# Seven products for all of the output projection: operand sums on GpSimd, weight sums by adding DMAs

## The chip, the cores and the metric

The kernel runs on one core of a Trainium2 chip. The metric is the device time of one execution in microseconds (us), as the median of several runs. The core has five engines that run their own instruction streams and meet at semaphores: TensorE (PE in the profile; its weight loads are listed apart as PEld) multiplies matrices into PSUM, VectorE (DVE) and ScalarE (ACT) work on tiles in SBUF and PSUM, GpSimd (POOL) does elementwise work and issues DMAs, and SyncE (SP) issues DMAs only. A DMA moves data between device memory (DRAM) and SBUF, or from DRAM to DRAM; an accumulating DMA adds what it reads to what stands at its destination.

## The reference

One layer of a decoder on 512 tokens with 2048 channels, all in fp32. Two mixers work on the normalised input, A (sparse attention) and B (a gated MLP over chunks). The change lies behind them:

```python
merged = g_a * (o_a @ w_up_a[l]) + g_b * (o_b @ w_up_b[l])
x = x + merged @ w_out[l]                                            # the output projection
x = x + jax.nn.sigmoid(x @ w_ple_gate[l]) * (p[l] @ w_ple[l])
return rms_norm(x, final_g)
```

`merged` is 512 x 2048 and `w_out` 2048 x 2048.

## The kernel before, in words

**Precision.** Each fp32 operand is held as two parts, a rounded one ("high", made by ACT at L147) and the rest ("low", the subtraction on VectorE at L153). A product of two operands is three matmuls: high by high, high by low, low by high.

**Jobs.** All large matrix products are jobs of one list, and the generator `gemm()` works through them in the order of the list, one matmul group at a time. `fill(n)` lets it do n groups, `finish(name)` lets it run until that job is done; between such calls the program text issues other work (loads, transposes, stores). There are plain jobs (kinds "T" and "N") and jobs of kind "S", which compute a product of 2 x 2 blocks in seven block products instead of eight (Strassen's scheme). In an "S" job of the projection's size the blocks are: two halves of the tokens, two halves of the 2048 inputs (16 k-tiles of 128, so 8 per half), and two column blocks of 512 that start at `c0` and `c2`. The products are named "1" to "7". Each needs a sum or difference of blocks of the activations (by `sum_part` for products 5, 6, 3, and with a third sum for product 7; the text calls them first, second, third and fourth sums) and of the weights (for products 5, 7, 6 and 4). Their results are added in PSUM banks where they can be, and on VectorE where not.

I call a *piece* the 12 matmuls of one product and one pair of k-tiles: two k-tiles, two token tiles of 128, three matmuls each. A product of the projection has four pieces, an "S" job 28. The inner matmuls of an "S" job are L377 to L379, those of an "N" job L415 to L417.

**Order ahead of a piece.** Before each piece (or each pair of k-tiles of a plain job) `gemm()` calls `flush()`, which issues the work put off in `deferred`; then `split_to()`, which issues ACT's high and VectorE's low of the weights up to two pieces ahead (`state["ahead"]`, into rings of three tiles, `hs` and `ls`); then `pop()`, which takes steps from two queues: `background` (small pieces of vector work, at a rate of `state["pops"]` per piece) and `slow` (DMAs that sum weights in DRAM, at a rate of 0.6 per piece). Every engine executes its instructions in the order in which this program issues them; no scheduler reorders them.

**DMA queues.** SP's queue carries the weights alone, 512 KB each, into rings of 3, 4 and 4 buffers (`rings`: raw, b11, b12). All other transfers are issued on GpSimd's queue, between GpSimd's own work.

**The jobs in time.** The mixers' projections come first, with the attention (its scores from 220 to 474 us) in the same TensorE stream. Four jobs m0 to m3 (721 to 1038 us) make the merge gates from `w_in`, ua0/ua1 and ub0/ub1 (to about 1195 us) the two up-projections. ub0 and ub1 read weight sums from DRAM (`up_sums`), which 32 DMAs on GpSimd's queue have made early (`up_sum`, L1141 to L1157: a copy of one block, then an accumulating DMA of the other; from the `slow` queue). At the end of ub0 and ub1, `final_up` (L816 on VectorE, L817 on GpSimd) forms the merged rows.

**Around the change.** `turn_merged(i, banks, n)` (L1713, transposes at L1724) turns the merged rows of half i into the layout that the projection needs, in four steps of eight transposes; each step takes two PSUM banks by letter, gives their highs to ACT and their lows to VectorE (L155), and then lets `gemm()` do n groups. wo0 and wo1 are the "N" jobs of the projection's first 1024 columns, 512 each; their results are added to the residual x by `add_x` (L833). wo2 is an "S" job of the other 1024 columns; the differences of its weights are formed by VectorE (L271). The sums of its activations are made by `sum_chunk` (L1480) on VectorE, as background steps during wo0 and wo1; the third sums go to DRAM (`s3_dram`) and are read back by `load_s3`. As each 512 columns of the new x are done, `store_x2` writes them to DRAM and `turn_x2` transposes them for the next product with `w_ple_gate` (jobs pg0 to pg3). Two parts of the order, in the main sequence:

```python
    finish("ub1")
    fill(4)
    turn_merged(1, "gs", 4)
    ...
    finish("wo0")
    store_x2(0)
    fill(6)
    turn_x2(0, "to", stage, 8, third_sum(quad_places))
    load_x(1, new_x())
    finish("wo1")
```

## Time and profile before

| what | value |
|---|---|
| median of three runs | 1543.36 us (1542.88 to 1543.55) |
| the profiled execution | 1543.99 us, its span 1541.9 us |
| granted TensorE clock, mean | 0.998 |
| busy: PE / PEld / DVE / ACT / POOL | 1527.2 / 1278.5 / 1225.7 / 807.8 / 312.5 us |
| DMA | 298.61 MB, mean 194 GB/s |
| wo0 and wo1, 1194.9 to 1287.0 us: PE / DVE / ACT / POOL | 92.10 / 71.75 / 38.02 / 19.86 us of 92.10 |
| wo2, 1287.0 to 1366.9 us: PE / DVE / ACT / POOL | 79.83 / 64.03 / 37.76 / 11.98 us of 79.90 |

How to read it: the span runs from the first to the last instruction of one profiled execution; the execution's own time is 2.1 us longer. A busy time counts how long an engine executed instructions; matmuls overlap in TensorE's pipeline, so the duration of one (0.39 us) is longer than the distance to the next. Lines name an engine, a line of the kernel (often that of a helper such as `low`), the operation, and the tiles written and read. An arrow names what ended a wait.

### The profile page before, as it was taken

What the parts mean: (1) busy time and instruction counts of PE and PEld (TensorE: products, weight loads), DVE (VectorE), ACT (ScalarE), POOL (GpSimd) and SP (SyncE); (2) the same over time, 40 slices, a digit from 0 to 9 for tenths busy, and PEclk for the clock granted to TensorE, in tenths of its full rate; (3) what the DMA queues carried; (4) which work ended last, traced back from release to release, by engine and by line L of the source; (5) the groups of instructions that cost most, each with busy time, mean ns of one, the idle gap of its engine ahead of it and who ended that gap; (6) DMA issues with size and microseconds to landing.
All of it is one profiled execution on the core that took longest, in us unless ns stands there. A gap on an engine that the chain in (4) does not pass through costs nothing.

```text
span 1541.9 us, 20629 instructions
## 1 busy us (share of the span) xinstructions
PE 1527.2 (99%) x7390; PEld 1278.5 (83%) x7390; DVE 1225.7 (79%) x1901; ACT 807.8 (52%) x1369; POOL 312.5 (20%) x494
## 2 busy tenths in 40 slices
PE   9999999999999999999999999999999999999997
PEld 7889988888888888888888888888888888888886
DVE  6548758888887888978988787787888786978877
ACT  6534446666665555545545445455545343444556
POOL 1201121212223233301122132230123221100000
PEclk9999999999999999999999999999999999999999
DMA  8426754356548884917474646686875487454555
GB/s 311 143 82 189 232 132 112 103 106 171 118 138 225 285 283 133 287 55 245 150 276 132 237 137 231 223 275 237 296 291 177 137 264 228 157 198 167 188 205 191
DMA packets 175846, 298.61 MB, mean 194 GB/s; under 512 B 11240, under 2 KB 88704, under 8 KB 172544
## 3 DMA queue, kind: packets, MB, share of 16 engines
q1 hardware_dynamic: 117456, 157.96, 31.4%
q0 software_dynamic: 58144, 139.07, 29.7%
q8 instruction: 58, 0.95, 0.2%
q14 instruction: 44, 0.36, 0.1%
q10 hardware_dynamic: 144, 0.26, 0.0%
HBM read 235.91 MB, written 78.12 MB: 204 GB/s over the span
## 4 chain that ended last, share of the span: by engine, by line
PE 92%; DVE 4%; ACT 1%; issue 1%; DMA 1%; SPq 0%; POOL 0%; DVEq 0%; ACTq 0%; POOLq 0%
PE ps_m L378 6%; PE ps_m L379 6%; PE ps_m L377 6%; PE ps_za L403 2%; PE ps_t L1240 2%; PE ps_za L404 2%; PE ps_za L405 2%; PE ps_wo L417 2%; PE ps_wo L415 2%; PE ps_wo L416 2%; PE ps_pg L378 2%; PE ps_wo L378 2%; PE ps_pg L377 2%; PE ps_pg L379 2%; PE ps_ua L378 2%; PE ps_zb L379 2%
## 5 line engine op out<-in xcount | busy, mean ns | idle before, releaser
L153 DVE TENSOR_TENSOR ls<-b,hs 128x1024 fp32r<-128x1024 f32 x210 | 262.0, 1248 | 106.5 <-ACT hs L147 104.7
L147 ACT CAST hs<-b 128x1024 fp32r<-128x1024 f32 x210 | 220.7, 1053 | 239.3 <-PE ps_m L379 65.5
L153 DVE TENSOR_TENSOR lo<-raw,hi 128x512 fp32r<-128x512 f32 (+1 forms) x184 | 125.7, 689 | 55.2 <-issue 18.6
L147 ACT CAST hi<-raw 128x512 fp32r<-128x512 f32 (+1 forms) x184 | 109.1, 603 | 87.9 <-PE ps_wo L417 19.4
L147 ACT CAST hs<-raw 128x1024 fp32r<-128x1024 f32 x94 | 99.0, 1054 | 104.2 <-PE ps_m L379 28.6
L153 DVE TENSOR_TENSOR ls<-raw,hs 128x1024 fp32r<-128x1024 f32 x94 | 116.9, 1244 | 24.3 <-ACT hs L147 24.3
L377 PE MATMUL ps_m<-hs,act_h 128*128 128x512 f32 x256 | 100.5, 393 | 0.0
L378 PE MATMUL ps_m<-ls,act_h 128*128 128x512 f32 x256 | 99.9, 390 | 0.2 <-DVE ls L153 0.2
L379 PE MATMUL ps_m<-hs,act_l 128*128 128x512 f32 x256 | 99.7, 389 | 0.0
L271 DVE TENSOR_TENSOR b<-raw,b 128x1024 f32<-128x1024 f32 x80 | 97.4, 1218 | 2.1 <-DMA raw<-in_w_in_dram 1.5
L271 DVE TENSOR_TENSOR b<-b,b 128x1024 f32<-128x1024 f32 x80 | 97.4, 1218 | 0.0
L147 ACT CAST pth<-ps_t 128x512 fp32r<-128x512 f32 (+1 forms) x88 | 48.0, 545 | 65.7 <-PE ps_t L1240 65.4
L1201 ACT ACTIVATE prob<-prob,st 128x512 f32<-128x512 f32 (+3 forms) x128 | 70.7, 556 | 4.0 <-DVE st L1192 3.8
L153 DVE TENSOR_TENSOR ptl<-ps_t,pth 128x512 fp32r<-128x512 f32 (+1 forms) x88 | 56.1, 638 | 20.8 <-ACT pth L147 20.0
L1192 DVE CUSTOM_DVE_ANT_0 prob<-ps_s,b 128x512 f32<-128x512 f32 (+3 forms) x128 | 56.3, 486 | 9.9 <-PE ps_s L1189 9.7
L378 PEld LDWEIGHTS ps_m<-ls,act_h 128*128 128x128 f32 x256 | 48.1, 188 | 10.7 <-DVE ls L153 1.0
L379 PEld LDWEIGHTS ps_m<-hs,act_l 128*128 128x128 f32 x256 | 48.1, 188 | 10.0
L377 PEld LDWEIGHTS ps_m<-hs,act_h 128*128 128x128 f32 x256 | 48.1, 188 | 9.8
L403 PE MATMUL ps_za<-act_h,hi 128*128 128x512 f32 x128 | 55.8, 436 | 0.0
L403 PE MATMUL ps_q<-act_h,hi 128*128 128x512 f32 x128 | 53.6, 419 | 0.0
L1240 PEld LDWEIGHTS ps_t<-ident,prob 128*128 128x128 f32 x320 | 39.7, 140 | 13.9 <-DVE ptl L153 3.0
L1240 PE MATMUL ps_t<-ident,prob 128*128 128x128 f32 x320 | 49.4, 273 | 1.4 <-DVE ptl L153 1.3
(686 smaller groups left out, 4463.8 us busy)
## 6 DMA issues: line engine op xcount, KB each, us to landing
raw<-in_w_in_dram SPq DMA_DIRECT2D x112, 512.0 KB, 4.3
b<-in_w_in_dram SPq DMA_DIRECT2D x56, 512.0 KB, 5.5
t<-in_w_up_b_dram POOLq DMA_DIRECT2D x24, 512.0 KB, 7.3
raw<-in_w_out_dram SPq DMA_DIRECT2D x24, 512.0 KB, 3.8
raw<-in_w_ple_gate_dram SPq DMA_DIRECT2D x24, 512.0 KB, 3.8
act_l<-gate POOLq DMA_DIRECT2D x8, 1024.0 KB, 10.5
hsum<-h_stage POOLq DMA_DIRECT2D x12, 512.0 KB, 4.3
gate<-keep POOLq DMA_DIRECT2D x24, 256.0 KB, 3.7
```

Of the source, the lines that this page charges most:

```text
L147: nc.scalar.copy(hi, src)
L153: nc.vector.tensor_tensor(out=lo, in0=src, in1=hi.bitcast(F32), op=ALU.subtract)
L271: nc.vector.tensor_tensor(out=b[o], in0=b[x], in1=b[y], op=ALU.subtract)
L377: nc.tensor.matmul(o, ah, wh, start=st, stop=False, skip_group_check=go)
L378: nc.tensor.matmul(o, ah, wl, start=False, stop=False, skip_group_check=go)
L379: nc.tensor.matmul(o, al, wh, start=False, stop=sp, skip_group_check=go)
L403: nc.tensor.matmul(ps, hi[:, j], ah, start=st, stop=False)
L404: nc.tensor.matmul(ps, hi[:, j], al, start=False, stop=False)
L405: nc.tensor.matmul(ps, lo[:, j], ah, start=False, stop=sp)
L1192: nc.vector.tensor_tensor_reduce(out=pt[:, j * n:j * n + n], in0=o[:, j], in1=b0[:, 512 - n:], scale=-SLOPE[h], scalar=3.0e38, op0=ALU.add ...
L1201: nc.scalar.activation(sl, sl, AF.Exp, bias=st[:, 0, j, hh:hh + 1], scale=-1.0, accum_out=st[:, 1, j, hh:hh + 1])
L1240: nc.tensor.transpose(b[:, (2 * e + hh) * P:(2 * e + hh + 1) * P], pts[hh][:, c:c + P], ident)
```

## The change

The first 1024 columns of the projection are computed by seven products too. The jobs wo0 and wo1 become one "S" job wo0 with column blocks at 0 and 512, in an order of its own (`LATE`) and with four pairs of PSUM banks instead of three (`LATE_BANK`); since a bank may now be opened by any product, `gemm()` works out for each bank which product begins it. Products 1 and 2 come first, product 3 last.

Both projection jobs get `sums`: the weight sums are read from DRAM (`out_sums`). `weight_sum` replaces `up_sum` and makes them for ub0, ub1, wo0 and wo2, as 96 DMAs on GpSimd's queue instead of 32. They stand in the `slow` queue from earlier on, and are taken from it at a rate of 0.8 per piece early, none while the sums of h are made, 0.85 in the attention, then none again, and 0.34 in m0 to m3. VectorE's weight differences in wo2 (L271 of the kernel before) go.

The sums of the activations are made by `merged_sums` in place of `sum_chunk`. 28 operations of 128x512 run on GpSimd (`gp`): 8 for the whole rows (two of the four `whole` steps while ub1 ends, two in wo0), 4 third sums, 8 first and 8 fourth; VectorE keeps the four second sums and the lows of all the results. They are spread over wo0 by a table of its 28 pieces (`plan`). The store of the third sums and `load_s3` go.

The order of the program changes around it. `turn_merged(1)` stands after `fill(2)` and uses the two banks "o" in all four steps, where it used "g" and "s". `turn_x2(0)` moves from wo1 into wo2. The second quarter of x is held as four tiles, stored block by block at wo0's end, and read back from `x2_dram` for `turn_x2(1)`.

```diff
+        self.bank_of = bank_of or BANK_OF
+        self.begins = {b: next(p for p, _ in products(self) if self.bank_of[p] == b) for b in set(self.bank_of.values())
+                       } if kind == "S" else None
...
+LATE = [(p, j) for p, js in (("1", "0123"), ("2", "2301"), ("4", "012"), ("7", "012"), ("6", "0123"), ("7", "3"),
+                             ("5", "0123"), ("4", "3"), ("3", "0123")) for j in map(int, js)]
+LATE_BANK = {"1": 0, "7": 0, "6": 1, "5": 1, "3": 1, "2": 2, "4": 3}
...
     def pop():
-        state["late"] += 0.6
+        state["late"] += state["rate"]
...
-                    b = BANK_OF[p]
+                    b = job.bank_of[p]
+                    begins = job.begins[b] == p
+                    pieces = [i for q, i in products(job) if q == p]
+                    opens, closes = j == pieces[0], j == pieces[-1]
...
-    s3_dram = dram.tile([P, 2, 8, 256], F32R, name="s3_d")
+    out_sums = [{p: dram.tile([P, 8, 512], F32, name=f"o{p}{i}") for p in "5674"} for i in range(2)]
...
-    for cg in range(2):
-        add_job(Job(f"wo{cg}", "N", w_out, 512 * cg, 512, KT, h_act, evac_out(cg), (ys, xs)[cg]))
+    def evac_out(p, ps):
+
+        for cg, row in {"1": ((0, 0), (1, 0)), "2": ((0, 0),), "7": ((0, 2), (1, 2)), "4": ((0, 2),),
+                        "6": ((0, 2),), "5": ((1, 2),), "3": ((1, 0),)}[p]:
+            for t in range(2):
+                add_x(cg, row + t, ps[t])
+        if p == "4":
+            later(lambda: store_x2(0))
+        elif p in "53":
+            for t in range(2):
+                later(lambda t=2 * (p == "5") + t: nc.gpsimd.dma_start(x2_dram[block(t, 512)], x_tiles[1][t]))
+
+    add_job(Job("wo0", "S", w_out, 0, 512, KT, part_act, evac_out, ("t", "g", "s", "o"), order=LATE, bank_of=LATE_BANK,
+                sums=out_sums[0]))
     add_job(Job("wo2", "S", w_out, 1536, 512, KT, part_act,
-                evac_quad(lambda t, c, o, src: add_x(2 if c else 3, t, src), tiles=False), ("o", "t", "s"), c2=1024))
+                evac_quad(lambda t, c, o, src: add_x(2 if c else 3, t, src), tiles=False), ("o", "t", "s"), c2=1024,
+                sums=out_sums[1]))
...
+    def weight_sum(job, q, p, first, second):
+
+        ks = slice(2 * q, 2 * q + 2)
+        o = job.sums[p][:, ks]
...
+        return [lambda: nc.gpsimd.dma_start(o, of(first)),
+                lambda: nc.gpsimd.dma_start(o, of(second), accum_op=ALU.add)]
+
+    summed = [j for j in jobs if j.sums]
+    for group in (summed[0:2], summed[2:3], summed[3:4]):
+        for p, first, second in (("5", "b12", "b11"), ("7", "b22", "b12"), ("6", "7", "b11"), ("4", "6", "b21")):
+            chains = [weight_sum(job, q, p, first, second) for job in group for q in range(job.kt // 4)]
+            for step in range(2):
+                slow.extend(c[step] for c in chains)
...
+        def gp(o, x, y, op):
+            x, y = (i.bitcast(F32) if i.dtype == F32R else i for i in (x, y))
+            nc.gpsimd.tensor_tensor(out=o, in0=x, in1=y, op=op)
...
+        def whole(c):
+            wholes[c] = ring(c, F32).rearrange("p a (h t) -> p (a h) t", h=2)
+            k1, _, a21, a11 = halves(c)
+            for o, t in ((a21, hi_t), (a11, lo_t)):
+                gp(o, act_h(k1, t), act_l(k1, t), ALU.add)
...
+        def first(c):
+            _, k2, s1, _ = halves(c)
+            gp(s1, act_h(k2, hi_t), s1, ALU.subtract)
+            gp(s1, s1, act_l(k2, hi_t), ALU.add)
+
+        def second(c):
+            _, _, s1, s2 = halves(c)
+            add(s2, s2, s1)
...
+        plan = [[] for _ in range(28)]
+        for c in range(4):
+            if c < 2:
+                plan[c].append(partial(whole, c))
+            plan[2 + c // 2].append(partial(third, c))
+            for f, piece in ((first, 5), (parts_7, 7), (second, 11), (parts_of_sum("6", 3, -1.0), 12),
+                             (parts_of_sum("5", 2), 14)):
+                plan[piece + c].append(partial(f, c))
+            plan[17 + c // 2].append(partial(fourth, c))
+            plan[21 + c].append(partial(parts_of_sum("3", 2), c))
...
+    state["rate"] = 0.34
...
+    whole, plan = merged_sums()
+    background.extend(partial(whole, c) for c in (2, 3))
     finish("ub1")
-    fill(4)
-    turn_merged(1, "gs", 4)
...
     load_x(0, new_x())
+    x_tiles[1] = [stream.tile([P, 512], F32, tag="hi", name="x_1", bufs=4) for _ in range(TT)]
+    for t in range(TT):
+        nc.gpsimd.dma_start(x_tiles[1][t], x[block(t, 512)])
+    background.extend(plan)
+    fill(2)
+    turn_merged(1, "oo", 4, 2)
     finish("wo0")
-    store_x2(0)
-    fill(6)
-    turn_x2(0, "to", stage, 8, third_sum(quad_places))
-    load_x(1, new_x())
-    finish("wo1")
     assert not background
-    store_x2(1)
-    load_s3()
-    fill(4 * 8)
+    fill(8)
+    turn_x2(0, "gg", stage, 4, third_sum(stream_places))
+    load_x(1, new_x(), x2_dram)
+    fill(4 * 4)
     turn_x2(1, "gg", lambda k, b: split(ob_h[:, k], ob_h[:, 4 + k], b, later=True), 4,
```

More of the change, by code (lines that the diff above doesn't have):

```diff
@@ L226 @@
     raw, parts = {}, {}
-    state = {"loads": 0, "sum": 0, "high": 0, "low": 0, "ahead": 0, "more": 1, "pops": 2, "due": 0, "b11": 0, "late": 0}
+    state = {"loads": 0, "sum": 0, "high": 0, "low": 0, "ahead": 0, "more": 1, "pops": 2, "due": 0, "b11": 0, "late": 0, "rate": 0.8}
     def ring(i, dtype, n=2):
@@ L357, in gemm @@
                 sets = {}
-                quad["spare"] = {"o": "g", "g": "o", "s": "o"}[job.banks[0]]
+                quad["spare"] = {"o": "g", "g": "o", "s": "o", "t": "o"}[job.banks[0]]
                 half = job.kt // 2
@@ L370, in gemm @@
                         k = 2 * j + i
-                        st, sp = k == 0 and p in "152", k == half - 1
+                        st, sp = begins and not i and opens, i == 1 and closes
                         for t in range(2):
@@ L381, in gemm @@
                                 yield
-                    if k == half - 1:
+                    if closes:
                         job.evac(p, sets[b])
-                    if p == "4" and k == half - 1:
+                    if (p, j) == products(job)[-1]:
                         done.add(job.name)
@@ L1138 @@
     state["pops"] = 2
[L1141 to L1158 removed]
+    state["rate"] = 0.85
     ph_b = ph_ab.enter_context(ExitStack())
@@ L1412 @@
     finish("za7")
-    assert not slow
+    state["rate"] = 0
     for _ in range(2):
@@ L1550 @@
         background.extend(oa_chunk(c))
-    def load_s3():
-        for k in (slice(2 * q, 2 * q + 2) for q in range(4)):
-            for i, a in enumerate((act_h, act_l)):
-                nc.gpsimd.dma_start(a(k, hi_t), s3_dram[:, i, k])
     finish("vn")
@@ L1668 @@
     finish("m3")
-    assert not background
+    assert not background and not slow
     ph_mix.close()
@@ L1711, with turn_merged @@
     load_gate_b(0)
-    def turn_merged(i, banks, n):
+    def turn_merged(i, banks, n, wait=0):
         for cg in (2 * i + 1, 2 * i):
@@ L1734, in turn_merged @@
                     split(act_h(k + e), act_l(k + e), b, 0.5, later=True)
-                fill(n)
+                fill(n + wait * (j == 2 and cg % 2))
     finish("ub0")
```

107 lines of the change are left out of this document (42 added, 65 removed).

## The prediction

> **What bounds the kernel now.** I read the page first, then TensorE's waits in the second half, then busy time by stretch, then both sides of one boundary in the timeline.
>
> ```profile
> span 1541.9 us, 20629 instructions
> PE 1527.2 (99%) x7390; PEld 1278.5 (83%) x7390; DVE 1225.7 (79%) x1901; ACT 807.8 (52%) x1369; POOL 312.5 (20%) x494
> ```
> ```profile
> PE ps_ub L378 <- DVE ls L153: 0.4, 1, 0.4
> ```
> ```profile
> 380.00:390.00 10.00, 10.00 (x58) 8.54 (x58) 7.38 (x23) 6.39 (x15) 1.44 (x2) 1.00 0.20 54
> 390.00:400.00 10.00, 10.00 (x58) 8.64 (x58) 9.70 (x26) 7.28 (x19) 2.42 (x5) 1.00 0.61 102
> 900.00:1000.00 100.00, 99.77 (x462) 82.84 (x461) 77.96 (x77) 49.33 (x60) 26.94 (x46) 1.00 0.66 214
> 1140.00:1150.00 10.00, 10.00 (x46) 8.27 (x45) 10.00 (x9) 3.35 (x5) 7.81 (x4) 1.00 0.62 209
> 1194.90:1287.00 92.10, 92.10 (x432) 76.84 (x431) 71.75 (x110) 38.02 (x65) 19.86 (x23) 1.00 0.71 228
> 1287.00:1366.90 79.90, 79.83 (x369) 66.22 (x369) 64.03 (x70) 37.76 (x49) 11.98 (x18) 1.00 0.54 172
> ```
> (Columns: length; then PE, weight load, DVE, ACT, POOL busy; granted clock; share of the DMA engines; GB/s.)
>
> TensorE issues all the time: 99% of the span, clock 1.00, and in 1100 to 1370 us it waited once, 0.4 us, for VectorE's low half of a weight. A product that disappears is therefore worth its whole issue time; anything that makes TensorE wait is paid in full. The exposed spot is VectorE: 10.00 of 10.00 us at 1140, when GpSimd is busy for 7.81.
>
> ```profile
> 1194.87 0.39 PE L415 MATMUL ps_wo<-hi,act_h 128*128 128x512 f32 x1
> 1197.36 0.39 PE L417 MATMUL ps_wo<-hi,act_h 128*128 128x512 f32 x1
> 1197.60 1.03 PE L1724 MATMUL ps_m<-ident,act_h 128*128 128x128 f32 x8
> 1198.39 0.48 PE L415 MATMUL ps_wo<-hi,act_h 128*128 128x512 f32 x1
> ```
> ```profile
> 1185.86 1.21 DVE L153 TENSOR_TENSOR ls<-raw,hs 128x1024 fp32r<-128x1024 f32 x1
> 1188.20 2.32 DVE L153 TENSOR_TENSOR ls<-b,hs 128x1024 fp32r<-128x1024 f32 x1
> 1190.44 1.77 DVE L153 TENSOR_TENSOR lo<-raw,hi 128x512 fp32r<-128x512 f32 x1
> 1192.14 1.27 DVE L718 TENSOR_TENSOR keep<-ps_ub,keep 128x512 f32<-128x512 f32 x2
> 1193.34 0.68 DVE L153 TENSOR_TENSOR lo<-raw,hi 128x512 fp32r<-128x512 f32 x1
> 1195.67 3.01 DVE L816 SCALAR_TENSOR_TENSOR act_l<-act_l,keep 128x512 f32<-128x512 f32 x2
> 1201.57 1.29 DVE L155 SCALAR_TENSOR_TENSOR act_l<-ps_m,act_l 128x512 fp32r<-128x512 f32 x2 [1.18 <-POOL act_h L817]
> ```
> ```profile
> 1181.99 3.91 POOL L817 TENSOR_TENSOR act_h<-act_h,act_l 128x512 f32<-128x512 f32 x2 [19.79 <-DVE act_l L816]
> 1187.75 3.91 POOL L817 TENSOR_TENSOR act_h<-act_h,act_l 128x512 f32<-128x512 f32 x2 [1.85 <-DVE act_l L816]
> 1195.16 6.38 POOL L817 TENSOR_TENSOR act_h<-act_h,act_l 128x512 f32<-128x512 f32 x4 [3.49 <-DVE act_l L816]
> ```
> ```profile
> L817 POOL TENSOR_TENSOR act_h<-act_h,act_l x16: 1291/1737/2282, 1140.0 to 1199.8; 128x512 f32<-128x512 f32 x16
> ```
>
> The reader should see two things. Twelve matmuls from 1194.87 start their last at 1197.36: (1197.36 - 1194.87) / 11 = 0.2264 us per matmul. I call 12 matmuls a piece: 2.72 us. Eight transposes take 0.8 us. And a VectorE operation whose two inputs lie in SBUF loses 1.1 us beside a GpSimd sum (1.21 to 2.32, 0.68 to 1.77), while one that reads PSUM (L718) does not. A GpSimd sum itself goes from 1.29 us to 1.74 or 2.28.
>
> [...]
>
> **The change, part by part.**
>
> *Products.* wo0 and wo1 are 384 matmuls; seven products of four pieces are 336. 48 x 0.2264 = 10.9 us less TensorE. The 32 transposes of the merged rows and those of turn_x2 are moved, not removed. So wo0 lasts 28 x 2.72 + 32 x 0.1 = 79.5 us where the two jobs took 92.1.
>
> *VectorE and ACT inside wo0.* Spacings in the rows: 1.14 us for a 128x1024 low, 0.6 for a 128x512 operation. Per piece there is one low of 1.14: 28 make 31.9 us. PSUM evacuations 18 x 0.6 = 10.8 (8 before), transposed rows 8 x 0.6 = 4.8, lows of the operand sums 16 x 0.6 = 9.6, sums left on VectorE 4 x 0.6 = 2.4, the previous job's last gates 4 x 0.6 = 2.4. Together 61.9 of 79.5 us: alone it fits. A low is asked for two pieces ahead with three buffers, so VectorE may be about 2.9 us late (two pieces, 5.4, less 1.05 for ACT's cast and 1.14) before TensorE waits. ACT needs 28 x 1.05 + 24 x 0.6 = 44 us and fits.
>
> *GpSimd's sums.* 28 new 128x512 operations (L1512 in the changed file): 8 whole, 4 third, 8 first, 8 fourth; the 16 old ones (L817) stay. Three places matter, in the order of the built program.
>
> First, the boundary ub1 to wo0. Two whole sums now stand between the second and third pair of L817, where VectorE is already full: two more blocked operations, 2.2 us. VectorE also makes three 1024-wide lows here instead of one and two 512-wide ones, 1.1 us more; 0.4 us of waiting is there to absorb it. So it reaches the last gates 2.9 us later, and one low of 1.14 us instead of 0.6 follows. The first low of the transposed rows overwrites the tile that L817 reads; before, it waited for that (1.18) and ended at 1202.25. Now it ends at 1202.25 + 2.9 + 0.5 = 1205.7. Before, nobody cared: the transposes used the banks g and s in turn. Now all four steps use the two o banks, so the second step needs that low. It comes due after 0.7 us (a late low, which TensorE waits for in ub1) and half a piece, a transposing step and a piece: 1194.9 + 0.7 + 1.36 + 0.8 + 2.72 = 1200.4. Wait: 5.3 us, with the 0.7 about 6.0. Lower end, if the two whole sums block nothing: the low at 1202.25 against 1199.8, 2.4 us. Upper end 6.5, with 1.29 per block. I take 5.9, the value with the blocks as in the rows.
>
> Second, pieces 4 to 11. GpSimd then has 16 sums in a row, from about 1208.4, after the last L817 and five DMA issues. Alternating with VectorE each takes 1.8 us or so, until 1237. VectorE's work from piece 4's low on is 8 lows, 6 PSUM evacuations, 4 PSUM lows and 3 small lows, 17 us; 12 blocks at 1.1 add 13, together 30 us in 8 pieces, 21.8 us, and TensorE is delayed by what is left of the 8 us after its 2.9 of slack and some 1 us from the boundary's wait: about 4.2. Ends: 0 (sums falling beside the PSUM operations, which do not block) and 6.
>
> Third, the eight fourth sums from piece 17, where VectorE also has six evacuations: 8 blocks at most, 8.8 us, of which three fall beside PSUM operations; pieces 19 to 21 carry only one low each and take most of the rest back. 1.5 us, ends 0 and 3.
>
> *Sums that left VectorE.* In wo2, 16 weight subtractions of 1.22 us go (19.5 us), and in wo0 28 operand sums. TensorE did not wait for either, so this gains nothing by itself; it gives room. Cover: none needed.
>
> ```profile
> L271 DVE TENSOR_TENSOR b<-raw,b x8: 1214/1216/1219, 1300.6 to 1356.6; 128x1024 f32<-128x1024 f32 x8
> L833 DVE TENSOR_TENSOR x<-x,ps_wo x8: 680/684/689, 1242.4 to 1287.5; 128x512 f32<-128x512 f32 x8
> L1152 POOL DMA_DIRECT2D t<-in_w_up_b_dram x16: 1128/1154/1558, 221.9 to 479.7; - x16
> t<-in_w_up_b_dram POOLq DMA_DIRECT2D x24, 512.0 KB, 7.3
> b<-in_w_out_dram SPq DMA_DIRECT2D x8, 512.0 KB, 12.2
> x<-in_x_dram POOLq DMA_DIRECT2D x3, 1024.0 KB, 6.1
> L1592 POOL DMA_DIRECT2D mix_v<-vl_d x8: 757/766/787, 774.6 to 982.9; - x8
> L1606 PE MATMUL ps_sv<-mix_v,mix_w x64: 270/275/275, 784.2 to 999.5; 128*128 128x128 f32 x64
> DMA to landing us min/median/max: 3.2/4.8/8.3
> ```
>
> *Weight sums by DMA.* 96 transfers instead of 32, all on POOL's queue: 13 move ahead of the attention's operand sums, 49 stand in the attention, 34 among m0 to m3's loads and stores. An issue costs POOL at most 1.15 us: 64 x 1.15 = 74 us more in 900 us where POOL is about a quarter busy, and no TensorE instruction follows it closely but ps_sv, behind its mix loads: 784.2 - 774.6 = 9.6 us, landing 4.8, at most 8.3. An added issue ahead of it (1.15) fits. Traffic: an accumulating one, issued at 389, lifts the DMA share from 0.20 to 0.61 over 10 us, at most 4.1 us of all engines; a copy no more. In m0 to m3 34 such are at most 139 us in some 290, and the share 0.66 would come near 1. Weight loads have seven or more buffers there. I take 0, ends 0 and 5.
>
> *Loads and stores of the projection.* 56 weight loads of 512 KB instead of 32, one per 2.72 us, about 190 GB/s; a ring of seven asks some 15 us ahead against landings of 4 to 12. The 16 DMAs of the third sum go. The second quarter's residual is now read back from DRAM between turn_x2(0) and turn_x2(1), five pieces, 13.6 us: POOL must first issue four stores that wait for VectorE (about 4 us), then 6.1 to land. 0, ends 0 and 2.6 (landing 12.2).
>
> **The sum.** The profiled execution took 1543.99 us (2.1 around the span), 0.6 over the median of 1543.36. -10.9 + 5.9 + 4.2 + 1.5 + 0 + 0 = +0.7: 1544.7 on that execution, 1544.1 as a median. I say 1544.1. All lower ends: -10.9 + 2.4 = -8.5, 1534.9. All upper ends: -10.9 + 6.5 + 6 + 3 + 5 + 2.6 = +12.2, 1555.6.
>
> **Rivals.**
> A, the forecast: TensorE saves what VectorE's lateness gives back. 1544.1, its own range 1539.5 to 1547.5. For it: each blocked row above costs 1.1 us. Against: no row shows GpSimd sums for 28 us on end.
> B, VectorE keeps up. Only the first wait is there, and the long run of sums costs 1: -10.9 + 2.4 + 1 = 1535.9, to 1540 with half of the others. For it: 61.9 of 79.5 us leave 17.6 us, and only 0.4 us were lost at 1140 to 1160, where eight sums also fell in 20 us. Against: that stretch had slack on both sides.
> C, slower, VectorE is the bound of all wo0. 30 blocks at 1.1 make 33 + 61.9 = 94.9 us against 79.5; less 2.9, 12.5 us, and 2.9 from being late at the start: +4.5, 1547.9. It decides from 0.8 us per sum on: 24 + 61.9 + 2.9 - 2.9 - 79.5 = 6.4 would still be a gain of 4, at 0.95 it is even. [...]
> D, transfers. The DMA engines fill up in m0 to m3 or in wo2; eight ps_sv wait half a microsecond each and turn_x2(1) 2: 1544.1 + 6 = 1550.
>
> **How the numbers follow.** A 0.41, B 0.33, C 0.15 (a third of it the whole lock), D 0.11. 0.2% is 3.1 us, 1540.3 to 1546.4, about what a measurement tells from no change. A lies there for three quarters, the rest above; B is faster but for a little; C and D are slower. Faster 0.32, same 0.36, slower 0.32. Range 1535.5 to 1551: it leaves out the bottom of B and the tops of C and D.
>
> **What would show it.** TensorE's records: 48 matmuls fewer. A wait of 2.4 to 6 us in front of the second transposing step of the second merge turn, put down to a VectorE low or the GpSimd sum before it; waits of 1 to 2 us each for lows in pieces 6 to 11; VectorE above 95% busy in the first 45 us of wo0 with lows at 2.3 us. If those lows stay near 1.2, B holds; if VectorE is full to wo0's end, C; if TensorE waits in m0 to m3 or before turn_x2(1), D. The forecast is wrong if TensorE's waits in wo0 sum to under 6 or over 15 us.

## The result and the profile after

The changed kernel takes 1569.59 us as the median of four runs (1564.71 to 1573.49), the kernel before 1543.3 us beside it: a ratio of 1.0169, 95% interval 1.014 to 1.0198. It is 26 us slower where 1544.1 us was forecast, and outside the range. The runs also lie further apart, 8.8 us where those of the kernel before lie within 0.7. The profiled execution is the shortest of the four (1564.71 us), so what follows explains 21.1 us, the difference of the two spans.

The page of the changed kernel, its totals and its two large DMA queues (the second column of a queue is MB, the third its share of 16 engines):

```profile
span 1563.0 us, 20634 instructions
PE 1526.1 (98%) x7342; PEld 1272.3 (81%) x7342; DVE 1230.4 (79%) x1863; ACT 816.4 (52%) x1365; POOL 413.3 (26%) x577
q0 software_dynamic: 66960, 169.48, 37.9%
q1 hardware_dynamic: 119888, 170.55, 33.3%
```

The 48 matmuls are gone (7390 to 7342), but TensorE is busy for as long as before: the rest of them took longer. Its waits in the whole execution, without rows of under 0.5 us and without those that the kernel before has too (ps_t, ps_spin, ps_ub and ps_pl). Each row names the engine, what was to be written, the line and what ended the wait; then come us in total, times and longest:

```profile
PE ps_m L1771 <- DVE act_l L166: 5.0, 1, 5.0
PE ps_wo L392 <- DVE ls L164: 3.9, 3, 1.7
PE ps_m L392 <- DVE ls L164: 3.1, 7, 0.8
PE ps_b L1589 <- DMA bn<-in_sgu_b_dram: 2.7, 1, 2.7
PE ps_k L417 <- ACT hi L158: 2.7, 1, 2.7
PE ps_k L419 <- DVE lo L164: 1.7, 1, 1.7
PE ps_x L1815 <- DMA x<-x_d: 1.5, 1, 1.5
PE ps_sv L1652 <- DMA mix_w<-ws_d: 0.9, 1, 0.9
PE ps_wo L391 <- DVE x L849: 0.5, 1, 0.5
```

Five of these rows (for ps_m at L392, ps_b, ps_k twice and ps_sv) stand far ahead of the projection, where the kernel before waited for nothing longer than 1.4 us. The start of the first matmul of each group of jobs, taken from the listing of the profile by tile, divides the span into stages. All kernels run on the chip are in the table, so that the experiments below can refer to it (us per stage; a stage is named by its first job and the next stage's; vs-u is the attention, u-m0 holds the mixers' jobs from u to zb; the labels are those of the experiments):

```
kernel   start-vs  vs-u   u-m0   m0-ua0  ua0-wo0  wo0-pg0  pg0-end  span
before     133.0   357.9  230.5  316.8    156.7    172.4    174.6   1541.9
after      139.6   357.9  234.9  322.5    157.2    176.5    174.4   1563.0
e1         131.4   357.7  230.5  316.8    157.2    180.6    174.8   1549.0
e2         141.7   358.0  231.3  316.8    157.2    179.8    174.5   1559.3
e3         138.4   357.9  232.0  318.3    157.2    178.4    174.4   1556.6
e4         132.1   357.7  230.5  316.8    157.2    175.9    174.5   1544.7
e5         132.1   357.7  230.5  316.8    157.2    179.6    174.6   1548.5
e6         131.8   357.7  230.5  316.8    160.6    173.4    175.2   1546.0
e7         132.0   357.8  230.4  316.8    156.7    165.6    174.5   1533.8
e8         132.1   357.7  251.3  318.7    157.2    178.8    174.4   1570.2
e9         132.1   357.6  230.6  316.8    156.6    170.8    174.5   1539.0
e10        132.2   360.1  230.5  319.3    157.2    177.6    174.4   1551.3
e11        131.4   358.4  230.5  318.8    156.6    166.3    174.4   1536.4
e12        131.8   364.4  230.6  316.8    156.6    166.3    174.4   1540.9
```

The loss of the changed kernel falls into two parts: +6.6, +4.4 and +5.7 us, 16.7 together, in three stages ahead of ub0, where only the weight sums' DMAs had changed; and +4.6 from ua0 to pg0, where the products should have saved 10.9.

**What a wait costs beside itself.** The timeline of TensorE around the first loss, and busy time by stretch (length; PE, weight load, DVE, ACT, POOL busy; granted clock; DMA share; GB/s), both of the changed kernel:

```profile
84.02 0.50 PE L417 MATMUL ps_k<-act_h,hi 128*128 128x512 f32 x1 [2.66 <-ACT hi L158]
86.47 0.79 PE L419 MATMUL ps_k<-act_h,lo 128*128 128x512 f32 x1 [1.72 <-DVE lo L164]
87.06 0.63 PE L417 MATMUL ps_k<-act_h,hi 128*128 128x512 f32 x1
...
91.33 0.61 PE L418 MATMUL ps_k<-act_l,hi 128*128 128x512 f32 x1
```
```profile
84.00:88.00 4.00, 2.27 (x6) 1.54 (x7) 2.50 (x4) 1.52 (x3) 3.51 (x3) 0.62 0.95 278
88.00:92.00 4.00, 4.00 (x11) 3.10 (x10) 0.72 (x2) 2.70 (x6) 0.00 (x0) 0.53 1.14 236
92.00:96.00 4.00, 4.00 (x23) 3.51 (x22) 2.26 (x5) 0.00 (x0) 0.00 (x0) 1.00 1.12 211
```

After the two waits the granted clock is 0.53, and ten matmuls from 87.06 to 91.33 lie 0.427 us apart instead of 0.227: 10 x 0.2 = 2 us more. The stage's 6.6 us are 4.4 of waits and some 2 at the lower clock. The changed kernel has three such stretches, each at a wait: from 85.0 to 91.8, from 515.0 to 518.4 and from 1221.7 to 1225.0 us, with a granted clock of 0.50 to 0.51. I estimate their cost as half of the time that TensorE was busy in them (5.3, 3.4 and 2.8 us), 5 to 6 us together. The kernel before shows no such stretch between its start and its tail. Of the three stretches the first is 6.8 us long and stands at two waits close together (2.66 and 1.72 us), the second 3.4 at a wait of 2.73, the third 3.3 at one of 5.01. What sets their length no run shows.

**Where the first two losses come from.** DMA issues between 36 and 100 us, first of the kernel before, then of the changed one (count, KB each, median us from issue to landing):

```profile
raw<-in_w_in_dram SPq DMA_DIRECT2D x10, 512.0 KB, 3.4
```
```profile
t<-in_w_up_b_dram POOLq DMA_DIRECT2D x15, 512.0 KB, 10.9
raw<-in_w_in_dram SPq DMA_DIRECT2D x9, 512.0 KB, 10.6
```

The changed kernel starts ub0's and ub1's sums here, 15 DMAs in 45 us. A weight load then lands after 10.6 us instead of 3.4, and its ring has three buffers. ACT, which makes the highs, waits for these loads in the same 64 us, which it does not in the kernel before:

```profile
ACT hi L158 <- DMA raw<-in_w_in_dram: 23.5, 5, 10.1
```

In u the wait is for the load of a small bias tensor, 4 KB. The same view between 480 and 515 us:

```profile
o<-in_w_out_dram POOLq DMA_DIRECT2D x2, 512.0 KB, 8.6
bn<-in_sgu_b_dram POOLq DMA_DIRECT2D x1, 4.0 KB, 13.3
```

Two accumulating DMAs, issued at 491.5 and 497.3 us, stand ahead of it in GpSimd's queue, and it lands after 13.3 us (8.3 in the kernel before). In m0 to m3 VectorE waits for its own loads, which it did not in the kernel before; the lows queued behind are late, and TensorE waits for seven of them:

```profile
DVE v L1628 <- DMA v<-vn_d: 5.4, 3, 2.3
```

**The projection.** The timelines of VectorE and GpSimd in pieces 4 to 10 of the changed wo0:

```profile
1231.27 6.51 DVE L164 TENSOR_TENSOR ls<-b,hs 128x1024 fp32r<-128x1024 f32 x1
1237.70 2.47 DVE L849 TENSOR_TENSOR x<-x,ps_wo 128x512 f32<-128x512 f32 x4
1240.09 1.28 DVE L166 SCALAR_TENSOR_TENSOR act_h<-ps_m,act_h 128x512 fp32r<-128x512 f32 x2
1241.29 1.21 DVE L164 TENSOR_TENSOR ls<-raw,hs 128x1024 fp32r<-128x1024 f32 x1
1242.42 2.31 DVE L164 TENSOR_TENSOR ls<-b,hs 128x1024 fp32r<-128x1024 f32 x1
```
```profile
1230.42 1.29 POOL L1512 TENSOR_TENSOR sum<-b 128x512 f32<-128x512 f32 x1
1231.68 1.27 POOL L1512 TENSOR_TENSOR third<-b 128x512 f32<-128x512 f32 x1
1232.91 1.28 POOL L1512 TENSOR_TENSOR sum<-b 128x512 f32<-128x512 f32 x1
1234.16 1.29 POOL L1512 TENSOR_TENSOR third<-b 128x512 f32<-128x512 f32 x1
1235.42 1.27 POOL L1512 TENSOR_TENSOR b<-act_h,b 128x512 f32<-128x512 f32 x1
1236.77 2.16 POOL L1512 TENSOR_TENSOR b<-b,act_h 128x512 f32<-128x512 f32 x1
```

Lows beside a GpSimd sum last 2.31 us, as foreseen. One lasts 6.51: five GpSimd sums (the four third sums and the first sum behind them) run to their end at their undisturbed 1.27 to 1.29 us before it, and it ends only after GpSimd's small gap at 1236.7. The four operations that read PSUM at L849 take 2.47 us, 0.62 each, beside GpSimd sums, as long as four of them (L833) in the kernel before with no sum beside them (2.47 us at 1242.43): they are not slowed.

### The profile page after: what moved, and what is told of

It reads as the page before. It is cut to its first block, busy times and chain, and to the rows that moved or that the text cites. A ratio compares the mean times of both kernels' runs of the same rounds, so it can differ in the third digit from the quotient of the medians.

```text
span 1563.0 us, 20634 instructions
## 1 busy us (share of the span) xinstructions
PE 1526.1 (98%) x7342; PEld 1272.3 (81%) x7342; DVE 1230.4 (79%) x1863; ACT 816.4 (52%) x1365; POOL 413.3 (26%) x577
## 4 chain that ended last, share of the span: by engine, by line
PE 72%; issue 10%; DVE 8%; DMA 5%; POOL 2%; ACT 2%; SPq 0%; DVEq 0%; POOLq 0%; ACTq 0%
PE ps_m L392 5%; PE ps_m L393 5%; PE ps_m L391 5%; DVE ls L164 2%; PE ps_t L1266 2%; PE ps_wo L392 2%; PE ps_wo L391 2%; PE ps_wo L393 2%; PE ps_za L417 2%; PE ps_za L418 2%; PE ps_za L419 2%; PE ps_pg L392 2%; PE ps_pg L391 2%; PE ps_ua L392 2%; PE ps_ua L391 2%
## 5 line engine op out<-in xcount | busy, mean ns | idle before, releaser
L164 DVE TENSOR_TENSOR ls<-b,hs 128x1024 fp32r<-128x1024 f32 x218 | 282.2, 1295 | 115.7 <-ACT hs L158 114.2
L158 ACT CAST hs<-b 128x1024 fp32r<-128x1024 f32 x218 | 229.3, 1053 | 250.3 <-PE ps_m L393 66.0
L158 ACT CAST hs<-raw 128x1024 fp32r<-128x1024 f32 x114 | 120.1, 1054 | 138.4 <-PE ps_wo L393 29.9
L164 DVE TENSOR_TENSOR ls<-raw,hs 128x1024 fp32r<-128x1024 f32 x114 | 148.9, 1306 | 37.9 <-ACT hs L158 37.5
L164 DVE TENSOR_TENSOR lo<-raw,hi 128x512 fp32r<-128x512 f32 (+1 forms) x152 | 101.7, 675 | 37.0 <-issue 8.2
L158 ACT CAST hi<-raw 128x512 fp32r<-128x512 f32 (+1 forms) x152 | 89.4, 599 | 71.9 <-DMA raw<-in_w_in_dram 23.9
L392 PE MATMUL ps_m<-ls,act_h 128*128 128x512 f32 x256 | 100.3, 392 | 2.3 <-DVE ls L164 2.3
L393 PE MATMUL ps_m<-hs,act_l 128*128 128x512 f32 x256 | 99.7, 390 | 0.0
L282 DVE TENSOR_TENSOR b<-raw,b 128x1024 f32<-128x1024 f32 x72 | 87.7, 1218 | 0.2
L282 DVE TENSOR_TENSOR b<-b,b 128x1024 f32<-128x1024 f32 x72 | 87.7, 1218 | 0.0
L392 PEld LDWEIGHTS ps_m<-ls,act_h 128*128 128x128 f32 x256 | 48.1, 188 | 14.0 <-DVE ls L164 4.4
```

The costliest lines, as they stand in the source:

```text
L158: nc.scalar.copy(hi, src)
L164: nc.vector.tensor_tensor(out=lo, in0=src, in1=hi.bitcast(F32), op=ALU.subtract)
L282: nc.vector.tensor_tensor(out=b[o], in0=b[x], in1=b[y], op=ALU.subtract)
L392: nc.tensor.matmul(o, ah, wl, start=False, stop=False, skip_group_check=go)
L393: nc.tensor.matmul(o, al, wh, start=False, stop=sp, skip_group_check=go)
```

## The experiments

The first four divide the change. They leave out or shrink the projection's weight sums; wo0 and wo2 then read plain blocks of the weights of the same size.

**e1: the projection alone.**

```diff
-                    src = weights(job, k + 2 * j, 2, c) if p in "123" else job.sums[p][:, 2 * j:2 * j + 2]
+                    plain = p in "123" or job.w is w_out
+                    src = weights(job, k + 2 * j, 2, c) if plain else job.sums[p][:, 2 * j:2 * j + 2]
...
-    summed = [j for j in jobs if j.sums]
+    summed = [j for j in jobs if j.sums and j.w is w_up_b]
...
-"rate": 0.8}
+"rate": 0}
...
-    state["rate"] = 0.85
+    state["rate"], state["late"] = 0.6, 0
```

> The changed kernel without the 64 DMAs that sum the projection's weights (wo0 and wo2 read a plain block of w_out in the place of each sum, as many bytes on SP's queue), and with the 32 DMAs of ub0 and ub1 back in the attention at 0.6 per piece. So the change of the projection alone is left. If the transfers cost the 17 us that the changed kernel lost ahead of ub0: 1543.3 + 4.7 (lost from ub0 to wo2's end) = 1548, 1545 to 1551, and the runs close together again. If GpSimd's sums and the new order cost nearly all (rival): 1560 or more.

Measured: 1548.94 us (1547.21 to 1550.68), ratio 1.0041 (1.0026 to 1.0056). The first five stages are those of the kernel before within 2 us. So, between medians, 20.7 us of the 26 belong to the transfers of the sums, and some 6 to the projection. The runs lie 3.5 us apart, less than 8.8 but not as close as before.

**e2: e1 with the sums of ub0 and ub1 early.**

```diff
-"rate": 0}
+"rate": 0.8}
...
-    state["rate"], state["late"] = 0.6, 0
+    state["rate"] = 0.85
```

> As the run before, but the sums of ub0 and ub1 start early as in the changed kernel (0.8 per piece, 15 DMAs between 55 and 100 us, the rest at 0.85 in the attention). If those 15 starve the weight loads: 4.4 us of waits near 85 us and 2.2 us at half the granted clock behind them, so 6.6 more than the run before, about 1554.5. If the early wait has another cause: the same as the run before.

Measured: 1560.82 us (1556.29 to 1561.0). The cause holds, its size was too small: 11.9 us over e1. In this execution the two waits for ps_k were 2.7 and 2.8 us, and the stage took 10.3 us more than in e1: 5.5 of waits, and most of the rest at a granted clock of 0.50 from 89.7 to 99.7 us. Moving these 15 DMAs ahead of the attention is the dearest part of the transfers, 11.9 of 20.7 us between medians (6.6 of 16.7 in the changed kernel's profile).

**e3: all 96 DMAs, 64 of them small.**

```diff
...
-        o = job.sums[p][:, ks]
+        cols = slice(0, 32 if job.w is w_out else 512)
+        o = job.sums[p][:, ks, cols]
...
```

> The changed kernel with all 96 DMAs at their places, but each of the 64 for the projection moves 32 of its 512 columns, a sixteenth of the bytes in as many rows (wo0 and wo2 read plain blocks). If their bytes cost the 10 us lost in u and in m0 to m3: about 1554.5, like the kernel that leaves them out. If the places they take in GpSimd's queue and its time to issue them do: about 1565, with the wait for the bias load at the start of u and VectorE's waits for its loads in m0 and m1 still there.

Measured: 1558.31 us (1557.79 to 1558.92), 11.3 below the changed kernel and 2.5 below e2. Of the 10.1 us that the changed kernel lost in u and in m0 to m3, 3.0 are left (1.5 in each, by the table). So bytes, not places in GpSimd's queue or its time to issue, cost about 7 of the 10. The 3 left may be the queue's, or small transfers not being free; this run does not tell these apart.

**e4: two pairs of banks for the second merge turn, on e1.**

```diff
-                pair = [bank(banks[e], "ps_m") for e in range(2)]
+                pair = [bank(banks[j // 2], "ps_m") for e in range(2)]
...
-    turn_merged(1, "oo", 4, 2)
+    turn_merged(1, "og", 4, 2)
```

> The first of these runs (projection alone), with the second merge turn's steps in the banks o and g in turn, where all four used o. If the 5.0 us wait at its second step is the wait for the banks, it goes, and with it the 1.5 us or so that TensorE then ran at half the clock: 6.5 less than the first run, about 1541.5; 2 to 3 of it may come back as waits for VectorE's lows in pieces 2 to 8. If VectorE is simply behind by that much (rival): the wait moves to the next piece and the time stays within 1.5 of the first run.

Measured: 1546.6 us (1545.68 to 1549.82), 2.3 less than e1: between the two. TensorE's waits from 1180 to 1340 us in this run:

```profile
PE ps_wo L393 <- DVE ls L164: 6.7, 4, 5.0
PE ps_x L1816 <- DMA x<-x_d: 2.6, 1, 2.6
```

The wait for the banks is gone, and a wait of 5.0 us for a low has taken its place some pieces later: the low is again one that a run of GpSimd sums holds up (three third sums and the first sum behind them), for 5.01 us. In e1 the three waits for lows had come to 4.0 beside 5.0 for the banks. So the banks only decided where VectorE's lateness was paid; most of it is the same lateness.

The next three ask what makes VectorE late, all on e4 (so they too read plain blocks in the place of the weight sums).

**e5: the third sums on VectorE.**

```diff
-            gp(thirds[c], a11, a21, ALU.subtract)
+            sub(thirds[c], a11, a21)
```

> The run with the projection alone and the banks o and g in turn, with the four third sums on VectorE (0.6 us each) in the place of GpSimd. In that run, as in all with this change, one low on VectorE lasts 5 to 6.5 us beside four third sums that GpSimd runs back to back at 1.25 to 1.29 us each, and TensorE waits 4.98 us for it. If such a run of sums holds VectorE off until GpSimd has a gap: no low above 2.4 us, the 4.98 wait and the 1.95 us at a lower clock go, 1546.6 - 5.5 = about 1541 (1539.5 to 1543). If VectorE only has too much to do there (rival): 4 x 0.6 more of it, 1546.6 to 1549.

Measured: 1551.41 us (1550.32 to 1555.56), ratio to before 1.0061 (1.0046 to 1.0076): slower than e4 by 4.8, and above both expectations. No low lasts over 2.4 us now, against 5.01 in e4, so the run of the third sums did hold VectorE off; but taking it away gained nothing.

```profile
PE ps_wo L393 <- DVE ls L164: 8.2, 5, 3.9
```

TensorE waits 8.2 us for lows instead of 6.7, and behind two waits close together (3.9 and 2.6 us) its matmuls lose about 2.4 us more to a lowered clock than in e4 (an estimate: half of TensorE's busy time in the stretches at 0.50, 8.5 us here and 3.8 there). The rival is right in kind: VectorE has more to do there than time, and the 2.4 us of added work cost more than the one long block had.

**e6: all 28 sums on VectorE.** One word of `gp` changes, `nc.gpsimd` to `nc.vector`.

> As the run before, with all 28 operand sums on VectorE, GpSimd left with the 16 sums of the gates. 28 x 0.6 = 16.8 us more work on VectorE, 78.7 of 79.5 us in wo0 by the rows of the kernel before. If a GpSimd sum costs VectorE 1.1 us or more each time they meet, doing it itself costs less: 1540 to 1545. If GpSimd takes work off VectorE (rival): later than with GpSimd's sums, 1549 or more.

Measured: 1548.22 us (1546.01 to 1549.58), 1.6 over e4 and within the spread of both: neither expectation. The waits from 1180 to 1340 us that changed are the following.

```profile
PE ps_wo L393 <- DVE ls L164: 5.8, 3, 2.9
PE ps_ub L392 <- DVE keep L733: 2.1, 1, 2.1
```

28 sums on GpSimd cost the kernel about as much as on VectorE: GpSimd takes nearly nothing off it here. VectorE's busy times, behind the next run, show the same.

**e7: copies on ACT for the sums.** The 28 sums are left out; ACT copies the first operand of each.

```diff
-            nc.gpsimd.tensor_tensor(out=o, in0=x, in1=y, op=op)
+            nc.scalar.copy(o, x)
```

> As the run with the projection alone and the banks o and g in turn, with each of the 28 sums replaced by an ACT copy of its first operand (the sums are left out; 28 x 0.6 us on ACT): VectorE is neither blocked by these sums nor given them. If they are the cause of its lateness: TensorE's waits for lows in wo0 (6.7 us, and 1.95 at a lower clock) shrink to 1, so about 1538.5 (1537 to 1541). If the lows, evacuations and the gates' sums alone make VectorE late (rival): above 1543.

Measured: 1536.26 us (1534.79 to 1537.05), ratio 0.9957 (0.9942 to 0.9972), 10.3 less than e4.

```profile
PE ps_x L1816 <- DMA x<-x_d: 2.9, 1, 2.9
PE ps_wo L393 <- DVE ls L164: 0.5, 1, 0.5
```

With the sums out of VectorE's way, 0.5 us of waiting for lows is left of 6.7: the sums cause these waits. Busy time from ua0 to pg0 of e4, e6 and e7 (columns as above; VectorE's is the third busy time):

```profile
1037.10:1370.20 333.10, 322.34 (x1457) 264.41 (x1456) 266.02 (x272) 164.42 (x208) 109.93 (x92) 0.99 0.73 250
1036.80:1370.80 334.00, 322.85 (x1458) 265.58 (x1458) 266.77 (x300) 164.47 (x208) 58.97 (x64) 0.99 0.73 249
1036.90:1359.20 322.30, 318.45 (x1458) 263.67 (x1457) 248.09 (x272) 179.45 (x236) 59.00 (x64) 1.00 0.75 258
```

With the sums on GpSimd (e4) VectorE is busy for 17.9 us longer than without them (e7), though it executes the same 272 instructions; with the sums on VectorE (e6) for 18.7 us. The saving of the products shows too: from wo0 to pg0 165.6 us, less 3.4 for these two waits is 162.2, 10.2 below the 172.4 of the kernel before, where 10.9 was the sum.

The last five look for a place for the transfers, and for a version that is faster.

**e8: the whole change, its DMAs elsewhere.** The rate is 0 ahead of the attention, 1 in it up to three slots from its end, 0.6 from within u until m0 begins, 0 in m0, 0.3 after.

> The whole changed kernel with its 96 adding and copying DMAs at other times: none before the attention, 1 per piece in the attention up to three slots from its end, then 0.6 per piece from the end of the bias transposes in u to zb, none in m0 to m3. If where they fall decides: the waits at 85 us, for the bias load and in m0 and m1 all go, 1549 (1546 to 1552), the same as with the projection alone. If 33 us of all 16 DMA engines' time is simply too much wherever it stands (rival): 1556 or more, with new waits for weights in u to zb.

Measured: 1571.69 us (1570.31 to 1573.39): the expectation failed. The 33 us in its rival are too few: by the shares of the two large queues all 16 DMA engines were busy for 129 us longer in the changed kernel (71.2% of 1563.0 us) than in e1, without the 64 DMAs of the projection's weight sums (63.5% of 1549.0). All but one of the sums' DMAs were issued by 745 us, 50 of them by the attention's end and 45 from u to zb. Busy time of this run in two stretches, the attention and u to zb (columns as above):

```profile
131.00:490.00 359.00, 357.15 (x2071) 309.07 (x2070) 288.50 (x789) 214.68 (x555) 93.62 (x139) 1.00 0.69 173
490.00:720.00 230.00, 215.44 (x925) 175.07 (x925) 175.06 (x187) 109.43 (x136) 93.20 (x143) 0.97 1.00 282
```

Beside them the same stretches of the kernel before:

```profile
131.00:490.00 359.00, 357.27 (x2071) 309.09 (x2070) 287.99 (x791) 214.78 (x554) 77.04 (x120) 1.00 0.57 147
490.00:720.00 230.00, 229.62 (x1016) 189.54 (x1015) 191.06 (x203) 119.60 (x145) 57.50 (x105) 1.00 0.68 216
```

The attention took 50 DMAs at a share of 0.69 and no time. From u to zb a mean share of 0.68 had looked like nearly the same room as the attention's 0.57; with 45 more DMAs the engines are full (1.00) and 20.8 us are lost. So a mean share of 0.6 to 0.7 does not tell how much a stage can take. Why these two stages differ is open: the jobs from u to zb sum their weights on VectorE, from blocks that must both have landed, but no run tests whether that is the reason.

**e9: the whole sums by ACT from PSUM, on e4.**

The function is called in `turn_merged`, ahead of the split of the same banks.

```diff
         def whole(c, pair):
+            o = ring(c, F32)
+            wholes[c] = o.rearrange("p a (h t) -> p (a h) t", h=2)
+            for e, b in enumerate(pair):
+                nc.scalar.mul(o.rearrange("p a (h t) -> p a h t", h=2)[:, :, e], b.rearrange("p (a t) -> p a t", a=2), 0.5)
...
+                if not i:
+                    whole(k // 2, pair)
...
-            plan[2 + c // 2].append(partial(third, c))
+            plan[(2, 3, 0, 1)[c]].append(partial(third, c))
+            plan[(6, 8, 4, 10)[c]].append(partial(first, c))
...
```

> The run with the projection alone and the banks o and g in turn, with the eight whole sums of GpSimd gone: ACT copies them from PSUM, times 0.5, while the first merge turn has them there; the third and first sums then spread over pieces 0 to 10. Eight of GpSimd's 28 sums less beside VectorE's fullest stretch, no work given to VectorE. If GpSimd's sums are what makes VectorE late (with all of them as ACT copies 10.3 us went): 8/28 of 10.3 is 2.9, and more because the rest no longer runs back to back: 1541 (1538 to 1544). If the lateness is set by the first sums alone (rival): 1545.5 or more.

Measured: 1540.97 us (1538.87 to 1542.39), ratio 0.9986 (0.9977 to 0.9996), as expected. The row is high plus low of merged rows that ACT has just read from PSUM; taken there, it needs no second operand and no work of GpSimd or VectorE. The run also moves the third and the first sums to other pieces, so the 5.6 us that it gains over e4 belong to both. The waits for lows from 1180 to 1340 us:

```profile
PE ps_wo L393 <- DVE ls L164: 2.2, 3, 1.4
```

**e10: the whole change with 1.6 DMAs per piece in the attention** (80 of them; `pop()` issues two where the rate asks for it), 16 in m1 to m3.

> The whole changed kernel, with its 96 DMAs at 1.6 per piece in the attention (some 80 of them) and the rest at 0.2 per piece in m1 to m3. The run that moved them showed 50 in the attention at no cost and 46 in u to zb at 20.8 us. If the attention, whose plain jobs ask for less weight per us, has room for 80: 1550 (1547 to 1554), near the projection alone. If 50 was its limit (rival): 1558 or more, with waits for weights between 190 and 490 us.

Measured: 1552.4 us (1549.54 to 1552.99). 17.2 us of the change's 26 come back from moving transfers alone. By the table the attention took 2.4 us longer than in e1, and m0 to m3 2.5.

**e11: all of it together** (e10's transfers, e9's whole sums, e4's banks, `fill(22)` for `fill(4 * 4)` ahead of the second quarter's turn and `fill(18)` for `fill(4 * 6)` behind it).

> A version that computes all: the transfers of the run before, the whole sums by ACT and the banks o and g in turn as in the run with these, and the turn of the second quarter of x a piece and a half later, so that it does not wait for its load. Sum: 1541 for the projection, 2 for the 16 transfers left in m1 to m3, 2.6 less for the load: 1540.5 (1537 to 1546), a tie with the kernel before or a little faster. If the costs of the transfers come back in the attention: 1550 or more.

Measured: 1540.09 us (1537.11 to 1542.84), ratio 0.9983 (0.9974 to 0.9993): 2.7 us faster than the kernel before, a small gain that the interval holds. The wait for the load of x is gone, waits for lows in wo0 come to 1.7 us.

**e12: e11 with 2 per piece in the attention,** so that all 96 stand there.

> The version that computes all, with the 96 DMAs at 2 per piece in the attention, so that nearly none is left for m1 to m3. With 80 there, the DMA engines were busy for 0.87 of that stretch and TensorE's waits in it grew by about 0.3 us; the 16 behind it cost about 2 us in m1 to m3. If the attention has room for all: 1538 (1536.5 to 1539.5). If it is full at about 85 (rival): 3 us or more are lost between 190 and 490 us, in u or in waits of GpSimd's own steps, and the time is 1540 or more.

Measured: 1541.89 us (1540.32 to 1546.06), ratio 0.9997 (0.9988 to 1.0006): the rival. The attention's stretch in e11, then in e12:

```profile
131.00:490.00 359.00, 356.86 (x2068) 308.60 (x2067) 288.04 (x789) 214.66 (x553) 122.48 (x169) 1.00 0.87 217
```
```profile
131.00:490.00 359.00, 351.65 (x2037) 303.16 (x2036) 286.10 (x785) 212.49 (x550) 134.13 (x183) 1.00 0.96 240
PE ps_s L1214 <- ACT oc L1370: 3.6, 1, 3.6
```

At a share of 0.87 the attention lost 0.7 us against e1 (2.4 in e10, with the same 80 transfers and a share of 0.86), at 0.96 it lost 6.7, half of it in one wait for the attention's own steps. What was won in m1 to m3 (2.0 us) was lost there.

## Why the prediction was wrong

- **The step that failed: "Weight sums by DMA. ... I take 0, ends 0 and 5."** It cost 16.7 us in the profiled execution and 20.7 between the medians of the changed kernel and e1. The step read mean shares over long stretches (0.66 in m0 to m3) and counted buffers. Its own bound for m0 to m3, 139 us of all engines in some 290, would add 0.48 to 0.66, which is more than there is; it called this "near 1" and still priced it at nothing. The 34 transfers there cost 5.7 us, at a measured share of 0.87. It counted transfers ahead of the attention (13; the trace has 15, then 47 and 34) and gave them no price: beside the first weight loads they cost 6.6 us (11.9 in e2). And it did not see the last sums of the attention, ahead of the small load that u needs (4.4). Rival D had transfers as the cause, but only in m0 to m3 and wo2; its chance of 0.11 and its price of 6 us were too small.
- **A term that the sum did not have: the lower clock behind a wait.** The three stretches at 0.50 cost some 5 to 6 us, by the estimate above. The kernel before had no wait of over 1.4 us, so its profile could not show this.
- **Products, -10.9: right.** 48 matmuls fewer, and -10.2 in e7 with its waits taken off. wo0 (its 336 matmuls into ps_wo, up to the first of wo2) was to last 79.5 us without waits and lasts 80.5 in e7, 92.8 in the changed kernel.
- **The boundary's wait, 5.9: nearly right in place and size** (5.0 us at the second step of the merge turn, and about 1.4 at the lower clock behind it). But it was not an addition of its own to the next term: e4 took the bank wait away and gained 2.3 us, since the lateness of VectorE was paid a few pieces later.
- **Pieces 4 to 11, 4.2: 3.3 measured. Fourth sums, 1.5:** two waits of 0.5 and 0.6 us late in wo0, 1.1 in all. The price of 1.1 us per blocked low was right, but the worst low lost 5.3: several sums may pass it. The other price, a sum's whole 1.29 us (the end of 6.5 at the boundary, and "the whole lock" in C's chance), is shown by no run: in the changed kernel the lows from 1180 to 1320 us last at most 2.32 us, 1.1 over 1.21, but for the one of 6.51. e7 shows that the sums make nearly all of these waits: without them they shrink from 6.7 us in e4 to 0.5.
- **Reading x back, 0 with an end of 2.6:** a wait of 1.5 us in the changed kernel and 2.0 to 3.3 in the experiments that leave it as it is. The 3.5 us of slack that I counted (13.6 less 4 and 6.1) were not there.
- **"In wo2 ... it gives room"** holds, and the room was worth nothing, as said: wo2 lasts 82.0 us in e11, where TensorE waits for nothing in it, against 80.0 in the kernel before. Some 1.6 of the 2.0 are the 16 transposes of `turn_x2(0)` that moved into it, at the 0.1 us each of the prediction.
- **Two readings of rows were wrong.** The row for "one that reads PSUM (L718) does not" starts at 1192.14, between two GpSimd sums and beside none (one ends at 1191.66, the next starts at 1195.16); the statement itself holds, as L849 above shows. And "An issue costs POOL at most 1.15 us" takes the median of that row for its maximum, 1.558.
- **The signs.** The 48 matmuls, the wait at the second transposing step and the waits for lows came as announced, and VectorE was busy for 93% of wo0's first 45 us. The waits in wo0 come to some 9.5 us, inside the 6 to 15 that were to bear the forecast out: that sign looked at the projection alone, and most of the loss lay ahead of it. The sign for D, waits in m0 to m3, appeared.
- For the projection alone the forecast was +0.7 us; e1 shows +6 as a median. The clock's part (some 4 us: stretches at 0.50 behind the banks' wait and behind the load of x) and the load of x (3.0) make up most of that.

The waits in the list, 22.0 us, and the lower clock, less the products, come to some 17 of the 21.1 us; the rest is not traced. Open too is why the runs of the changed projection lie 3 to 5 us apart, even where the transfers are left out (e1, e4, e9), when those of e7 lie within 2.3. The clock is one candidate, as the last section suggests; it was not tested.

## What to carry to other kernels

A mean share of the DMA engines is no measure of room: put added transfers into a stretch a few at a time and look at the landing time of the loads beside them; here one stretch took 80 at a mean share up to 0.87 for 0.7 to 2.4 us, and another with 0.68 to begin with lost 20.8 us to 45. GpSimd is no spare engine for elementwise sums while VectorE is full of operations with two SBUF inputs (28 sums cost about the same on either here: 1546.6 us in e4, 1548.2 in e6, and 1536.3 without them in e7); a sum that ACT can take from PSUM costs neither (with eight of them there, and the others spread, the waits for lows fell from 6.7 to 2.2 us in e9). A wait of 2 to 5 us on a TensorE that never waited is priced with the clock that it may lose, here 1.4 to some 3 us more (estimates from the stretches at 0.50), but nothing behind 2.9 us in e7 and 3.6 in e12.

## What was unexpected of the hardware

**One low held off by several sums.** In each run with the four third sums back to back on GpSimd (the changed kernel, e1 to e4, e8, e10), with a first sum behind them, one low of VectorE lasted 5.0 to 6.5 us, while the sums ran undisturbed at 1.25 to 1.29 us; in e5, e6, e7, e9, e11 and e12, where they are elsewhere or apart, none lasted over 2.4. The prediction priced a low beside a sum at 1.1 us, and at most at the whole of one sum, 1.29. Here one low lost 3.8 to 5.3 us over its 1.21, as much as three to four sums. In the changed kernel and in e4 the sums beside it follow each other without a gap, and it ends 1.1 us behind the first gap of 0.08 us between two of them (at 1236.69 and at 1220.14 us). Whether the gap is what lets it through was not tested.

**The clock falls after one wait and not after another of its length.** Two waits for the load of x, about as long: 3.0 us in e1, 2.9 us in e7. Busy time in the stretches in which each ends, e1 first:

```profile
1312.00:1316.00 4.00, 2.63 (x11) 2.46 (x12) 0.00 (x0) 1.24 (x3) 0.00 (x0) 0.54 1.13 384
1316.00:1320.00 4.00, 4.00 (x14) 3.14 (x13) 3.08 (x5) 1.43 (x3) 0.00 (x0) 0.60 0.37 136
```
```profile
1300.00:1304.00 4.00, 2.94 (x17) 2.62 (x18) 0.90 (x2) 2.28 (x5) 0.00 (x0) 1.00 1.12 388
```

After the one the granted clock is 0.54 and 0.60, after the other 1.00. The length of the wait does not decide it: behind 2.0 us for the same load in e3 the clock was 0.50 from 1323.1 to 1326.3 us, and behind the 3.6 us in e12's attention it stayed at 1.00. What it takes for the clock to fall stays open.
